# Retention fetches the next head pair ahead, and the output projection's first tiles take the contraction row by row

## The chip, the cores and the metric

The kernel runs on one core of a Trainium2 chip. The metric is the device time of one execution in microseconds (us), given as the median of several runs. The engines named below are PE (TensorE, the matmuls), DVE (VectorE), ACT (ScalarE), POOL (GpSimd) and SP (SyncE, whose queue issues nearly all transfers).

## The reference, cut to what matters

Two layers work on 256 context tokens and 512 latent tokens of width 1024. In each, one input projection feeds four mixers (RWKV, SSD, Hyena, retention) of width 512; each mixer's gated output is projected, weighted by a sigmoid gate of the layer's input, added up, and projected once more. The change touches retention and the output projection. Retention goes in chunks of 128 tokens, for 8 heads of 64, forwards and backwards:

```python
def step(s, inp):
    qc, kc, vc = inp
    att = jnp.einsum('bnhd,bmhd->bhnm', qc, kc) * inner
    y = jnp.einsum('bhnm,bmhe->bnhe', att, vc)
    y = y + jnp.einsum('bnhd,bhde->bnhe', qc, s) * xi[None, :, :, None]
    s = g_chunk[None, :, None, None] * s + jnp.einsum('bmhd,bmhe,hm->bhde', kc, vc, zeta)
    return s, y
```

q and k pass a rotary embedding before it; y passes a norm over each head and a SiLU gate behind it.

## The kernel before

**Dense work.** Every projection in fp32 is three matmuls: both factors are split into a high and a low part (`uh`, `ul` for the layer's input, `yh`, `yl` for a mixer's output, `whi`, `wlo` for a weight tile), and hi·hi, lo·hi and hi·lo are added in PSUM. The helper of L215 issues these "dense" matmuls; each works on 512 latent columns (`dl`) or 256 context columns (`dc`). A weight tile is fetched by L193 (`wraw`), its high part cast by ACT (L185), its low part made by DVE (L186).

**Who sets the order.** The code gives the work in program order; the tile framework's list scheduler fixes at build time the order in which each engine and queue runs it. Each engine then runs its list strictly in turn. Dense work of the merge, which stands behind retention in the code, is thereby put between the steps of the mixers; it needs weight tiles from SP's queue. Tiles with the same tag share a fixed number of buffers (`BUFS`), and a transfer into one waits until its last reader is done.

**Retention.** `ret` calls `ret_ct` for four pairs of heads, pair 0 to pair 3. A pair fetches q, k and v from DRAM (L477), turns q and k (L961 to L964 on DVE), transposes v and k on PE (`cen`, `ident`, L174), scales k (`kz`, L983 on DVE), makes the chunk states (`vt`·`kz` on PE, `S`, L1008 and L1011 on DVE), multiplies q by k on PE, weights the products (`att`, L1026 on DVE) and adds both parts up in PSUM (`sy`, L174). The head norm follows: a square on ACT, a matmul with `bones` (L386), DVE's L397 to L400, then the gate (L403) and the store of `yd` (L1040). Layer 0 does it for 768 tokens, layer 1 for 512 outputs. The merge of mixer 3 reads `yd` of all four pairs back.

**Output projection.** `outp` works in four column blocks j; each splits four weight tiles (`owh`, `owl`, the fourth in `whi`, `wlo`), and for each 128-row tile (six in layer 0, four in layer 1) adds 24 matmuls of 256 columns (L1284 to L1286) in one of three PSUM buffers `o`. DVE's L1289 (`ot`) reads such a buffer and frees it.

Of the kernel before, what the change touches and what calls it, by code (L numbers as in the profile page):

```python
# [17 lines left out]
T_LAT, T_CTX, T = 512, 256, 768  # L18
# [121 lines left out]
class K:  # L140
# [5 lines left out]
    def tile(self, pool, shape, dt=F32, tag=None, bufs=None):  # L146
        self.n += 1
        kw = {}
        bufs = bufs or self.BUFS.get(tag)
        if bufs is not None:  # L150
            kw["bufs"] = bufs
        return pool.tile(shape, dt, tag=tag, name=f"{tag}_{self.n}", **kw)

    BUFS = dict(KB=1, pc=2, late=1, y=1, bonus=1, gt=4, stc=10, S=6, att=2, zn=2, yh=1, yl=1,  mg=2, rt2=5, rt=2, st=5, E=3, m2=2, cbm=2, dd=2, xd=2, sd=1, yo=1, ub=2, hw=2, ha=2, heo=1,
                H=2, Hs=1, eo=1, eot=1, U=2, Yf=1, t1=1, ss=1, et=3, AR=3, KBt=2, vt=2, UV=2, Rs=1, Z=2, pcm=1, wraw512=2, whi512=3, wlo512=3, fg=3, fh=3, hx=3, fraw=1, xh=1, xl=1,
                ht=2, hsq=1, hnm=1, hss=4, uf=2, uc0=1, hn=6, ot=2, adr=4, adh=3, adl=3, owh=5, owl=5)
    PSUM_D = dict(dl=2, dc=1)
# [771 lines left out]
    def ret(self, l, need_ctx, p):  # L929
        tc, V, S, G = self.tc, self.V, self.S, self.G  # L930
        segs = [(0, 512), (512, 256)]
        osegs = segs if need_ctx else segs[:1]
        self.load_smask(p)
        ld = {}
        for n, sh in (("dif", [128, 2, 128]), ("xidx", [128, 2, 128]), ("zidx", [128, 2]), ("rope", [128, 2, 512])):
            ld[n] = self.tile(p, sh, F32, n)
            self.nc.sync.dma_start(out=ld[n][:], in_=self.a[n])
        Dm = self.tile(p, [128, 8, 128], F32, "Dm")
        D2 = self.tile(p, [128, 8, 128], F32, "D2")
        for d, t in ((0, Dm), (1, D2)):  # L940
            for h in range(8):
                S.activation(out=t[:, h, :], in_=ld["dif"][:, d, :], func=AF.Exp, scale=self.col("lgr", 8 * d + h))
            G.tensor_tensor(out=t[:], in0=t[:], in1=self.smask[:, d, :].unsqueeze(1).to_broadcast([128, 8, 128]), op=ALU.mult)
        V.tensor_tensor(out=Dm[:], in0=Dm[:], in1=D2[:], op=ALU.add)
        zeta = self.tile(p, [128, 2, 8], F32, "zeta")
        for d in range(2):
            S.activation(out=zeta[:, d, :], in_=self.col("lgr", 8 * d, 8), func=AF.Exp, scale=ld["zidx"][:, d:d + 1])
        gch = self.tile(p, [128, 8], F32, "gch")
        S.activation(out=gch[:], in_=self.col("lg", 0, 8), func=AF.Exp, scale=128.0)
        for ct in range(4):  # L950
            self.ret_ct(l, ct, need_ctx, p, segs, osegs, ld, Dm, zeta, gch)

    def ret_ct(self, l, ct, need_ctx, p, segs, osegs, ld, Dm, zeta, gch):
        V, S, G = self.V, self.S, self.G
        no = T if need_ctx else 512
        nch = 6 if need_ctx else 4

        def rope(x):
            sh = self.tile(p, [128, 512], F32, "rt")
            mask = [(i + 16) % 32 for i in range(32)]  # L960
            V.stream_shuffle(out=sh[:], in_=x[:, 0:512], mask=mask)  # L961
            V.tensor_tensor(out=sh[:], in0=sh[:], in1=ld["rope"][:, 1, :], op=ALU.mult)
            V.tensor_tensor(out=x[:, 0:512], in0=x[:, 0:512], in1=ld["rope"][:, 0, :], op=ALU.mult)
            V.tensor_tensor(out=x[:, 0:512], in0=x[:, 0:512], in1=sh[:], op=ALU.add)  # L964

        q = self.fetch(l, "rq", ct, no, p, "q")
        k = self.fetch(l, "rk", ct, T, p, "k")
        v = self.fetch(l, "rv", ct, T, p, "rt2")
        rope(q)
        rope(k)  # L970
        vt = self.tile(p, [128, 6, 128], F32, "vt")
# [1 line left out]
        for src, kind in ((v, 0), (k, 1)):  # L973
            for gq in range(2):
                ps = self.ps("s", [128, 3, 128])
# [37 lines left out]
        y = self.tile(p, [128, T], F32, "rt2")  # L1013
        for t0, n in osegs:
# [3 lines left out]
            for b in range(nb):  # L1018
                o = t0 + b * 128
# [3 lines left out]
            att = []  # L1023
# [232 lines left out]
    def outp(self, l, need_ctx, acc, ah, p, wp, done):  # L1256

        V, nc = self.V, self.nc
        no = T if need_ctx else 512
        nt = no // 128  # L1260
        lag = 2 if need_ctx else 0
        al = self.tile(p, [128, 8, T], F32R, "al")
        for oc in range(8):
            self.split(ah[:, oc, :no], al[:, oc, :no], acc[:, oc, :no], scale=0.5)
        gb = self.tile(p, [128, 2, D], F32, "gb")
        for s in range(2 if need_ctx else 1):
            g = self.modd[l].rearrange("(c s) x -> c s x", s=2)[:, s, :]
            nc.sync.dma_start(out=gb[:, s, :], in_=bass.AP(g.tensor, g.offset, [[0, 128]] + list(g.ap)))
        hn = [self.tile(p, [128, D], F32, "hn") for _ in range(nt)]
        for i in range(nt):  # L1270
            nc.sync.dma_start(out=hn[i][:], in_=self.h_in(l, i))
        for j in range(4):
            w = []
            for q in range(4):
                raw = self.tile(self.wpool, [128, 2, 256], F32, "wraw512")
                nc.sync.dma_start(out=raw[:], in_=self.a["out_w"][l, j, :, 2 * q:2 * q + 2])
                hi, lo = (self.tile(self.wpool if q == 3 else wp, [128, 2, 256], F32R, t) for t in (("whi512", "wlo512") if q == 3 else ("owh", "owl")))
                self.split(hi[:], lo[:], raw[:])
                w += [(hi[:, kk, :], lo[:, kk, :]) for kk in range(2)]
            for i in range(nt):  # L1280
                ps = self.pst("o", [128, 256])
                ac = slice(i * 128, (i + 1) * 128)
                for k in range(8):
                    self.P.matmul(ps[:], ah[:, k, ac], w[k][0], start=(k == 0), stop=False)  # L1284
                    self.P.matmul(ps[:], al[:, k, ac], w[k][0], start=False, stop=False)  # L1285
                    self.P.matmul(ps[:], ah[:, k, ac], w[k][1], start=False, stop=(k == 7))  # L1286
                t = self.tile(p, [128, 256], F32, "ot")
                cs = slice(j * 256, (j + 1) * 256)
                V.tensor_tensor(out=t[:], in0=ps[:], in1=gb[:, 0 if i < 4 else 1, cs], op=ALU.mult)  # L1289
                V.tensor_tensor(out=hn[i][:, cs], in0=hn[i][:, cs], in1=t[:], op=ALU.add)  # L1290
                if j == 3 and i >= lag:
                    done(i - lag, hn[i - lag])
        for i in range(nt - lag, nt):
            done(i, hn[i])
# [179 lines left out]
```

## Time and profile before

| | |
|---|---|
| median of 3 runs | 3001.47 us (2997.48 to 3002.77) |
| the profiled execution | 3006.24 us |
| its span, first to last instruction | 3004.4 us |
| mean granted TensorE clock | 0.978 |
| PE busy | 2841.8 us, 95% of the span |
| PE's weight loads busy | 2294.0 us, 76% |
| DVE busy | 1906.4 us, 63% |
| ACT busy | 1187.5 us, 40% |
| POOL busy | 456.7 us, 15% |

Spans and rows are of the profiled execution; 1.84 us of its time lie outside its span. Its time is 4.77 us above the median of the runs. Busy PE time holds matmuls that wait in the array's pipeline, and the clock is a share of 2.4 GHz: 0.50 means the level of 1.2 GHz.

### The profile page before, as it was taken

What the parts mean: (1) busy time and instruction counts of PE and PEld (TensorE: products, weight loads), DVE (VectorE), ACT (ScalarE), POOL (GpSimd) and SP (SyncE); (2) the same over time, 40 slices, a digit from 0 to 9 for tenths busy, and PEclk for the clock granted to TensorE, in tenths of its full rate; (3) what the DMA queues carried; (4) which work ended last, traced back from release to release, by engine and by line L of the source; (5) the groups of instructions that cost most, each with busy time, mean ns of one, the idle gap of its engine ahead of it and who ended that gap; (6) DMA issues with size and microseconds to landing.
All of it is one profiled execution on the core that took longest, in us unless ns stands there. A gap on an engine that the chain in (4) does not pass through costs nothing. (4 is left out here: it accounts for less than half of the span.)

```text
span 3004.4 us, 48440 instructions
## 1 busy us (share of the span) xinstructions
PE 2841.8 (95%) x18708; PEld 2294.0 (76%) x18708; DVE 1906.4 (63%) x3544; ACT 1187.5 (40%) x2109; POOL 456.7 (15%) x650
## 2 busy tenths in 40 slices
PE   7998999999999999999999989899999999999897
PEld 3787878787777887777778878777777788877677
DVE  3348575665636769876735446757576746787865
ACT  4643424333336323334532464334344443333432
POOL 2300202112010001210012230121212010021111
PEclk9999999999999999999999999899989999999999
DMA  6543213131216332233535354223222225333334
GB/s 195 192 135 105 96 64 97 63 104 45 92 56 228 122 124 79 87 112 121 169 123 172 97 196 144 74 79 116 71 99 81 70 83 170 124 105 101 123 118 138
DMA packets 164266, 343.24 MB, mean 114 GB/s; under 512 B 19105, under 2 KB 28130, under 8 KB 164036
## 3 DMA queue, kind: packets, MB, share of 16 engines
q1 hardware_dynamic: 164036, 340.15, 34.6%
q8 instruction: 147, 2.41, 0.3%
q14 instruction: 83, 0.68, 0.1%
HBM read 254.77 MB, written 83.74 MB: 113 GB/s over the span
## 5 line engine op out<-in xcount | busy, mean ns | idle before, releaser
L215 PE MATMUL dl<-uh,whi 128*128 128x512 f32 (+1 forms) x1520 | 621.6, 409 | 6.6 <-ACT fg L457 3.1
L215 PE MATMUL dl<-ul,whi 128*128 128x512 f32 (+1 forms) x1520 | 618.9, 407 | 2.6 <-DVE ul L379 2.5
L215 PE MATMUL dl<-uh,wlo 128*128 128x512 f32 (+1 forms) x1520 | 616.1, 405 | 2.3 <-DVE wlo L186 2.3
L185 ACT CAST whi<-wraw 128x512 fp32r<-128x512 f32 x452 | 278.2, 615 | 642.0 <-PE dc L215 281.8
L186 DVE TENSOR_TENSOR wlo<-wraw,whi 128x512 fp32r<-128x512 f32 x452 | 324.4, 718 | 290.1 <-ACT whi L185 251.6
L215 PEld LDWEIGHTS dl<-uh,wlo 128*128 128x128 f32 (+1 forms) x1520 | 288.2, 190 | 68.3 <-DVE wlo L186 4.4
L215 PEld LDWEIGHTS dl<-uh,whi 128*128 128x128 f32 (+1 forms) x1520 | 288.6, 190 | 67.0 <-ACT fg L457 3.9
L215 PEld LDWEIGHTS dl<-ul,whi 128*128 128x128 f32 (+1 forms) x1520 | 288.8, 190 | 62.3 <-DVE ul L379 6.5
L215 PE MATMUL dc<-uh,whi 128*128 128x256 f32 (+1 forms) x960 | 277.4, 289 | 6.1 <-DVE fg L446 3.1
L215 PE MATMUL dc<-ul,whi 128*128 128x256 f32 (+1 forms) x960 | 276.0, 288 | 1.9 <-DVE ul L379 1.9
L215 PE MATMUL dc<-uh,wlo 128*128 128x256 f32 (+1 forms) x960 | 274.3, 286 | 0.0
L215 PEld LDWEIGHTS dc<-uh,whi 128*128 128x128 f32 (+1 forms) x960 | 180.6, 188 | 22.6 <-DVE fg L446 4.4
L215 PEld LDWEIGHTS dc<-ul,whi 128*128 128x128 f32 (+1 forms) x960 | 180.4, 188 | 18.2 <-DVE ul L379 6.2
L215 PEld LDWEIGHTS dc<-uh,wlo 128*128 128x128 f32 (+1 forms) x960 | 180.2, 188 | 4.1 <-issue 1.1
L1252 POOL TENSOR_TENSOR acc<-acc,fg 128x512 f32<-128x512 f32 x72 | 92.5, 1294 | 502.9 <-DVE fg L1251 501.5
L728 DVE TENSOR_TENSOR Z<-cc,Z 128x256 f32<-128x256 f32 x80 | 33.8, 422 | 139.4 <-PE cc L174 138.8
L858 POOL TENSOR_TENSOR m<-smask,adl 128x512 fp32r<-128x512 f32 x24 | 34.0, 1415 | 537.2 <-DVE adl L186 410.1
L215 PE MATMUL dl<-yh,whi 128*128 128x512 f32 x256 | 104.0, 408 | 7.3 <-ACT yh L185 6.4
L215 PE MATMUL dl<-yl,whi 128*128 128x512 f32 x256 | 103.7, 406 | 2.6 <-DVE yl L186 2.6
L215 PE MATMUL dl<-yh,wlo 128*128 128x512 f32 x256 | 104.2, 408 | 0.0
L701 POOL COPY UV<-vt 64x128 f32<-64x128 f32 x192 | 76.7, 422 | 166.8 <-ACT vt L634 161.2
L713 ACT COPY Rs<-cc 64x256 f32<-64x256 f32 x96 | 35.3, 367 | 161.2 <-PE cc L174 160.3
(422 smaller groups left out, 5722.5 us busy)
## 6 DMA issues: line engine op xcount, KB each, us to landing
wraw<-in_w SPq DMA_DIRECT2D x248, 256.0 KB, 2.7
wraw<-merge_w SPq DMA_DIRECT2D x128, 256.0 KB, 2.7
adr<-ada_w SPq DMA_DIRECT2D x96, 256.0 KB, 3.6
wraw<-branch_w SPq DMA_DIRECT2D x64, 256.0 KB, 2.8
wraw<-out_w SPq DMA_DIRECT2D x32, 256.0 KB, 3.8
pdlw<-fg SPq DMA_DIRECT2D x16, 384.0 KB, 2.4
pdla<-fg SPq DMA_DIRECT2D x16, 384.0 KB, 2.9
hfd<-Hs SPq DMA_DIRECT2D x16, 384.0 KB, 2.9
```

The costliest lines, as they stand in the source:

```text
L185: (heng or self.S).copy(out=hi, in_=src) if heng is None else heng.tensor_copy(out=hi, in_=src)
L186: (leng or self.V).tensor_tensor(out=lo, in0=src, in1=hi.bitcast(F32), op=ALU.subtract)
L215: i = self.P.matmul(out[t0][:M, :n], w[:, kk, :], u[:, k, t0:t0 + n], start=(k == 0 and p == 0), stop=(k == nk - 1 and p == 2))
L701: G.tensor_copy(out=UV[hk, d], in_=vt[d][hk, slot[d] // 2, :].rearrange("p (h x) -> p h x", h=2))
L713: S.copy(out=Rs[hb], in_=Rp.t[hb])
L728: V.tensor_tensor(out=Zn[:], in0=Zp.t[:], in1=Z[:], op=ALU.add)
L858: eng.tensor_tensor(out=m2[:], in0=self.smask[:, d, :].unsqueeze(1).to_broadcast([128, 4, 128]), in1=ad[:, c, hs:hs + 4].bitcast(F32).unsq ...
L1252: G.tensor_tensor(out=acc[:, oc, t0:t0 + n], in0=acc[:, oc, t0:t0 + n], in1=g[:, t0:t0 + n], op=ALU.add)
```

## The change

In retention `ret` fetches q, k and v of pair 0, and those of pair n+1 ahead of the code of pair n. They have tags of their own: two buffers for q and for k, one for v. The tag `rt2` has four buffers instead of five. In `outp` the first three tiles of block j = 0 are written with the contraction index k outermost: rows k = 0 to 6 over the three tiles, then k = 7 tile by tile. For these PE keeps the order of the code. The arithmetic is the same.

```diff
-    BUFS = dict(... rt2=5, rt=2, ...
+    BUFS = dict(... rt2=4, q2=2, k2=2, v2=1, rt=2, ...
...
+        def get(ct):
+            return [self.fetch(l, nm, ct, n, p, tag) for nm, n, tag in (("rq", no, "q2"), ("rk", T, "k2"), ("rv", T, "v2"))]
+
+        nxt = get(0)
         for ct in range(4):
-            self.ret_ct(l, ct, need_ctx, p, segs, osegs, ld, Dm, zeta, gch)
+            qkv, nxt = nxt, get(ct + 1) if ct < 3 else None
+            self.ret_ct(l, ct, need_ctx, p, segs, osegs, ld, Dm, zeta, gch, *qkv)
...
-        q = self.fetch(l, "rq", ct, no, p, "q")
-        k = self.fetch(l, "rk", ct, T, p, "k")
-        v = self.fetch(l, "rv", ct, T, p, "rt2")
...
-            for i in range(nt):
-                ps = self.pst("o", [128, 256])
-                ac = slice(i * 128, (i + 1) * 128)
-                for k in range(8):
+            ahead = range(min(3, nt) if j == 0 else 0)
+            pss = {}
+            def rows(i, ks):
+                if i not in pss:
+                    pss[i] = self.pst("o", [128, 256])
+                ps, ac = pss[i], slice(i * 128, (i + 1) * 128)
+                for k in ks:
                     self.P.matmul(ps[:], ah[:, k, ac], w[k][0], start=(k == 0), stop=False)
...
+            if ahead:
+                with self.tc.manual_schedule(engines={mybir.EngineType.PE}):
+                    for k in range(7):
+                        for i in ahead:
+                            rows(i, [k])
+                    for i in ahead:
+                        rows(i, [7])
```

What this does to the engines' lists is seen at three places. The first is SP's queue in layer 1, from the fetch of pair 1 to the store of pair 0 (`q`, `k`, and `rt<-pdrv` are a pair's fetch, `wraw` weight tiles of the merge, `rt<-pdgr` the gate). Before:

```order
L477 DMA q_24674<-pdrq_24_92 128x512
L477 DMA k_24676<-pdrk_26_94 128x768
L193 DMA wraw_5112_26454<-merge_w 128x512
L193 DMA wraw_5117_26475<-branch_w 128x512
L193 DMA wraw_5121_26496<-merge_w 128x512
L477 DMA rt_4720_24670<-pdgr_34_102 128x512
L477 DMA rt_4723_24678<-pdrv_28_96 128x768
L193 DMA wraw_5124_26514<-merge_w 128x512
L193 DMA wraw_5129_26535<-branch_w 128x512
L1040 DMA yd_71<-rt_4711_24626 128x512
L193 DMA wraw_5133_26556<-merge_w 128x512
L477 DMA q_24803<-pdrq_24_92 128x512
```

And now, from v of pair 1 on (L1044 is the store, L1040 before):

```order
L477 DMA v_4691_24558<-pdrv_28_96 128x768
L477 DMA q_4724_24683<-pdrq_24_92 128x512
L477 DMA k_4725_24685<-pdrk_26_94 128x768
L477 DMA v_4726_24687<-pdrv_28_96 128x768
L477 DMA rt_4723_24679<-pdgr_34_102 128x512
L477 DMA q_4759_24812<-pdrq_24_92 128x512
L1044 DMA yd_71<-rt_4714_24635 128x512
L477 DMA k_4760_24814<-pdrk_26_94 128x768
L477 DMA v_4761_24816<-pdrv_28_96 128x768
L477 DMA rt_4758_24808<-pdgr_34_102 128x512
L1044 DMA yd_71<-rt_4749_24764 128x512
L193 DMA wraw_5112_26457<-merge_w 128x512
```

The five merge weight tiles that stood between the fetch of pair 1 and the store of pair 0 now stand behind the fetches of pairs 2 and 3 and the store of pair 1. Next is PE in layer 1, where pair 1 begins (`cen` and `ident` transpose v and k, `dl` rows are dense). Before, 35 dense rows run from the `bones` matmul of pair 0 to this place:

```order
L215 MATMUL dl_26435<-uh_15075,wlo_5114_26457 128x512
L215 MATMUL dl_26435<-uh_15075,whi_5113_26456 128x512
L174 MATMUL s_24693<-cen_116,rt_4723_24678 128x128 x3
L174 MATMUL s_24698<-cen_116,rt_4723_24678 128x128 x3
L174 MATMUL s_24703<-ident_112,k_24676 128x128 x3
L174 MATMUL s_24709<-ident_112,k_24676 128x128 x3
L215 MATMUL dl_26435<-ul_15076,whi_5113_26456 128x512
L215 MATMUL dl_26435<-uh_15075,wlo_5114_26457 128x512
L215 MATMUL dl_26474<-yh_26293,whi_5118_26477 128x512
L215 MATMUL dl_26474<-yl_26294,whi_5118_26477 128x512
L215 MATMUL dl_26474<-yh_26293,wlo_5119_26478 128x512
L174 MATMUL s_24722<-vt_24690,kz_4727_24691 128x128
```

And now, where pair 2 begins, from the last `sy` row of pair 1 on:

```order
L174 MATMUL sy_24765<-qx_4737_24727,S_24760 128x128
L174 MATMUL sy_24765<-qx_4738_24729,S_24739 128x128
L386 MATMUL s_24799<-rt_4755_24796,bones_114 128x512
L174 MATMUL s_24831<-cen_116,v_4726_24687 128x128 x3
L174 MATMUL s_24836<-cen_116,v_4726_24687 128x128 x3
L174 MATMUL s_24841<-ident_112,k_4725_24685 128x128 x3
L174 MATMUL s_24847<-ident_112,k_4725_24685 128x128 x3
L174 MATMUL s_24860<-vt_24828,kz_4765_24829 128x128
L174 MATMUL s_24865<-vt_24828,kz_4765_24829 128x128
L174 MATMUL s_24872<-vt_24828,kz_4765_24829 128x128
```

The dense rows ahead of the transposes and behind them are gone. From the first `sy` row of pair 0 to the first of pair 3, 183 dense rows stood in layer 1 before and 13 stand there now; the 170 others come behind pair 3. In layer 0 the pairs follow each other in the same way, but keep dense rows in between, except in pair 0: there 8 dense rows (6 of 512 columns, 2 of 256) stood between the q·k rows and the first `sy` row, 4 of 256 between the first two `sy` rows, 6 of 256 ahead of `bones`, and none stands there now. The third place is DVE in the output projection of layer 0, behind the last split of block 0 (`owl` are low parts for block 1). Before:

```order
L186 TENSOR_TENSOR wlo_2848_15140<-wraw_2846_15137,whi_2847_15139 128x512
L1289 TENSOR_TENSOR ot_15168<-o_15143,gb_15104 128x256
L1290 TENSOR_TENSOR hn_15107<-hn_15107,ot_15168 128x256
L186 TENSOR_TENSOR owl_15314<-wraw_2861_15311,owh_15313 128x512
L1289 TENSOR_TENSOR ot_15196<-o_15171,gb_15104 128x256
L186 TENSOR_TENSOR owl_15320<-wraw_2864_15317,owh_15319 128x512
L1290 TENSOR_TENSOR hn_15108<-hn_15108,ot_15196 128x256
L1289 TENSOR_TENSOR ot_15224<-o_15199,gb_15104 128x256
```

And now (L1310 and L1311 are `ot` and `hn`, L1289 and L1290 before):

```order
L186 TENSOR_TENSOR wlo_2848_15140<-wraw_2846_15137,whi_2847_15139 128x512
L186 TENSOR_TENSOR owl_15317<-wraw_2861_15314,owh_15316 128x512
L186 TENSOR_TENSOR owl_15323<-wraw_2864_15320,owh_15322 128x512
L1310 TENSOR_TENSOR ot_15221<-o_15145,gb_15104 128x256
L1310 TENSOR_TENSOR ot_15224<-o_15149,gb_15104 128x256
L1311 TENSOR_TENSOR hn_15107<-hn_15107,ot_15221 128x256
L1311 TENSOR_TENSOR hn_15108<-hn_15108,ot_15224 128x256
L1310 TENSOR_TENSOR ot_15227<-o_15153,gb_15104 128x256
```

The first `ot` stood ahead of both `owl` of the next block and stands behind them now; layer 1 has the same rows in the same two orders.

## Rows read from the trace of the kernel before

**Rows 1.** Stretches: from:to, length; busy us of PE, PEld, DVE, ACT, POOL; clock; DMA

```profile
1326.00:1418.00 92.00, 89.71 (x606) 73.84 (x604) 65.87 (x133) 39.82 (x74) 5.24 (x2) 1.00 0.38 127
2810.70:2892.50 81.80, 77.93 (x463) 60.65 (x462) 68.20 (x134) 30.08 (x45) 9.51 (x6) 1.00 0.34 108
2912.70:2919.60 6.90, 5.79 (x14) 4.58 (x15) 3.03 (x4) 1.24 (x2) 0.51 (x1) 0.51 0.64 196
2920.00:2937.90 17.90, 17.90 (x79) 14.55 (x78) 9.29 (x12) 3.73 (x6) 9.80 (x7) 1.00 0.59 177
```

**Rows 2.** What VectorE waited for, layer 0 retention, 1326 to 1425 us

```profile
DVE rt L961 <- DMA q<-pdrq: 8.6, 4, 4.1
```

**Rows 3.** SP's queue in layer 1 (start, us, line, transfer)

```profile
2811.29 0.33 SPq L193 DMA_DIRECT2D wraw<-merge_w  x1
2835.30 0.33 SPq L477 DMA_DIRECT2D q<-pdrq  x1
```

**Rows 4.** TensorE by line in layer 1, 2810.7 to 2892.5 us

```profile
L215 PE MATMUL dl<-uh,wlo 128*128 128x512 f32 x41 | 17.0, 415 | 0.0
L215 PE MATMUL dl<-yh,wlo 128*128 128x512 f32 x20 | 8.4, 422 | 0.0
```

**Rows 5.** Timeline of VectorE in layer 1, pair 0 to pair 1, and pair 3

```profile
2809.38 1.28 DVE L1026 TENSOR_TENSOR att<-s,Dm 128x512 f32<-128x512 f32 x2
2817.11 0.69 DVE L397 TENSOR_SCALAR rt<-s 128x512 f32<-128x512 f32 x1 [1.61 <-PE s L386]
2819.52 0.68 DVE L992 TENSOR_TENSOR qx<-q,xi 128x512 f32<-128x512 f32 x1
2823.74 0.68 DVE L400 TENSOR_TENSOR rt<-sy,rt 128x512 f32<-128x512 f32 x1
2830.03 1.95 DVE L983 TENSOR_TENSOR kz<-s,zeta 128x384 f32<-128x384 f32 x4 [2.50 <-PE s L174]
2832.84 1.09 DVE L1008 TENSOR_TENSOR S<-s,bones 128x256 f32<-128x256 f32 x3 [0.25 <-PE s L174]
2836.60 1.28 DVE L1026 TENSOR_TENSOR att<-s,Dm 128x512 f32<-128x512 f32 x2
2891.78 1.27 DVE L1026 TENSOR_TENSOR att<-s,Dm 128x512 f32<-128x512 f32 x2
```

**Rows 6.** TensorE in layer 1: twelve transposes of pairs 0 and 1

```profile
2792.41 2.93 PE L174 MATMUL s<-cen,rt 128*128 128x128 f32 x12 [1.51 <-DMA rt<-pdrv]
2827.83 1.50 PE L174 MATMUL s<-cen,rt 128*128 128x128 f32 x12
```

**Rows 7.** What TensorE waited for behind pair 3, 2892 to 2930 us

```profile
PE dl L215 <- ACT yh L185: 1.8, 1, 1.8
PE dl L215 <- DVE yl L186: 1.3, 1, 1.3
```

**Rows 8.** Timeline of TensorE in layer 0, pair 0

```profile
1346.70 0.51 PE L215 MATMUL dl<-uh,whi 128*128 128x512 f32 x1
1348.66 0.43 PE L174 MATMUL sy<-att,vt 128*64 128x128 f32 x2
```

**Rows 9.** Output projection, layer 0: TensorE's fourth tile, VectorE's first split

```profile
1632.34 0.28 PE L1284 MATMUL o<-owh,ah 128*128 128x256 f32 x1
1632.46 0.28 PE L1285 MATMUL o<-owh,al 128*128 128x256 f32 x1
1633.25 0.69 DVE L186 TENSOR_TENSOR owl<-wraw,owh 128x512 fp32r<-128x512 f32 x1 [2.59 <-ACT owh L185]
```

**Rows 10.** The same in layer 1, and TensorE's wait behind it

```profile
2953.20 0.28 PE L1284 MATMUL o<-owh,ah 128*128 128x256 f32 x1
2954.29 0.69 DVE L186 TENSOR_TENSOR owl<-wraw,owh 128x512 fp32r<-128x512 f32 x1 [2.76 <-ACT owh L185]
PE o L1284 <- ACT owh L185: 1.4, 2, 1.0
```

More of the change, by code (lines that the diff above doesn't have):

```diff
@@ L152, in tile @@
         return pool.tile(shape, dt, tag=tag, name=f"{tag}_{self.n}", **kw)
-    BUFS = dict(KB=1, pc=2, late=1, y=1, bonus=1, gt=4, stc=10, S=6, att=2, zn=2, yh=1, yl=1,  mg=2, rt2=5, rt=2, st=5, E=3, m2=2, cbm=2, dd=2, xd=2, sd=1, yo=1, ub=2, hw=2, ha=2, heo=1,
+    BUFS = dict(KB=1, pc=2, late=1, y=1, bonus=1, gt=4, stc=10, S=6, att=2, zn=2, yh=1, yl=1,  mg=2, rt2=4, q2=2, k2=2, v2=1, rt=2, st=5, E=3, m2=2, cbm=2, dd=2, xd=2, sd=1, yo=1, ub=2, hw=2, ha=2, heo=1,
                 H=2, Hs=1, eo=1, eot=1, U=2, Yf=1, t1=1, ss=1, et=3, AR=3, KBt=2, vt=2, UV=2, Rs=1, Z=2, pcm=1, wraw512=2, whi512=3, wlo512=3, fg=3, fh=3, hx=3, fraw=1, xh=1, xl=1,
@@ L949, in ret, with ret_ct @@
         S.activation(out=gch[:], in_=self.col("lg", 0, 8), func=AF.Exp, scale=128.0)
+        no = T if need_ctx else 512
+        def get(ct):
+            return [self.fetch(l, nm, ct, n, p, tag) for nm, n, tag in (("rq", no, "q2"), ("rk", T, "k2"), ("rv", T, "v2"))]
+        nxt = get(0)
         for ct in range(4):
-            self.ret_ct(l, ct, need_ctx, p, segs, osegs, ld, Dm, zeta, gch)
-    def ret_ct(self, l, ct, need_ctx, p, segs, osegs, ld, Dm, zeta, gch):
+            qkv, nxt = nxt, get(ct + 1) if ct < 3 else None
+            self.ret_ct(l, ct, need_ctx, p, segs, osegs, ld, Dm, zeta, gch, *qkv)
+    def ret_ct(self, l, ct, need_ctx, p, segs, osegs, ld, Dm, zeta, gch, q, k, v):
         V, S, G = self.V, self.S, self.G
@@ L1286, in outp @@
                     self.P.matmul(ps[:], ah[:, k, ac], w[k][1], start=False, stop=(k == 7))
+            if ahead:
[5 more added lines that the diff above has]
+                        rows(i, [7])
+            for i in range(nt):
+                if i not in ahead:
+                    rows(i, range(8))
+                ps = pss[i]
                 t = self.tile(p, [128, 256], F32, "ot")
```

## The prediction

> **What bounds the kernel now.** I read the windows view first. TensorE (PE) is the engine that everything waits for: in layer 0's retention it is busy 89.71 of 92.00 us, in layer 1 from the last `att` row of pair 0 to that of pair 3 it is busy 77.93 of 81.80 us, both at the full clock [rows 1]. So whatever the change saves by shorter waits of other engines, it can save in these stretches no more than PE's own idle time: 2.29 and 3.87 us. Next come the waits of DVE: it waited 8.6 us for q in layer 0 [rows 2]. That looks like the prize, but PE had dense rows to run meanwhile, so little of it was on the path. The lines view shows what covered it in layer 1: 3 x 41 + 3 x 20 = 183 dense matmuls [rows 4] of 0.2266 us each (79 in 17.90 us at the full clock [rows 1]), 41.5 us of the 77.93. Retention's own matmuls are the other 36.4 us, 12.1 us a pair. The work of the pair that PE waits for is DVE's, so its timeline comes last, below.
>
> **Layer 1: dense rows leave the pairs.** The lists show 170 of the 183 dense rows moved behind pair 3. They are not saved; they cost 170 x 0.2266 = 38.5 us there. What counts is how long a pair takes without them. DVE's own list for one pair, from its timeline [rows 5]: the block of `S`, its updates and `att` runs 2832.84 to 2837.88, 5.0 us; four `kz` 1.95 us; and 16 wide operations (eight of the two rotations, two `qx`, L397, L279 to L281, L400, L403), each 0.603 us (seven from 2819.52 to 2823.74), 9.65 us. Together 16.6 us, more than PE's 12.1. On top come waits: in pair 1 DVE waited 1.61 us ahead of L397, 2.50 ahead of `kz` and 0.25 ahead of `S` [rows 5], 4.4 us, because norm, transposes and state are a ring between PE, ACT and DVE. The rotations of the next pair, whose q and k are now there, fill part of these. A pair thus takes 16.6 to 21.0 us; I take 18.0, a third of the waits.
>
> PE then idles some 18.0 - 12.1 = 5.9 us in each pair, and its clock may fall. The trace has one such place: behind pair 3 PE waited 1.8 and then 1.3 us [rows 7], and the stretch behind it ran at a granted clock of 0.51, the level of 1.2 GHz [rows 1]. What that costs: twelve transposes took 1.50 us at the full clock and 2.93 at the low level [rows 6], 1.43 us more. I take one low stretch a pair, long enough for its 24 transposes: 2.9 us, so a pair of 20.9 us. The ends are none (18.0) and the whole of a pair's own matmuls: 12.1 us more, of which the 5.9 us of idle time can hide that much, so 24.2 to 30.1 us a pair.
>
> The Trainium skill, page "TensorE: Matmul & The Clock Gate", Part 1, calls the low level the default state, left by activity and fallen back into by idling. The rows behind pair 3 agree with it. By it alone the pairs would run wholly at 1.2 GHz, and the sum would be that of the second rival below.
>
> Against this stands a gain: the 3.1 us of waits behind pair 3 [rows 7] were there because merge 3 needs `yd` of pair 3 back and nothing else was left to run. With 38.5 us of dense rows in that place they go, and so does the low stretch: 14 matmuls were busy 5.79 us where 14 x 0.2266 = 3.2 us do, 2.6 us [rows 1]. Together 5.7 us.
>
> Sum for layer 1: 3 x 20.9 + 38.5 = 101.2 us against 81.8, +19.4, less 5.7: **+13.7**. With pairs of 18.0: 92.5, less 5.7, +5.0. At the least 3 x 16.6 + 38.5 = 88.3, +6.5 - 5.7 = +0.8. At the low level throughout +23.6 (24.2 us a pair) to +41.3 (30.1).
>
> **SP's queue.** The twelve fetches of a layer stay twelve; only their places change. Before, a weight tile left at 2811.29 and the fetch of pair 2 at 2835.30 [rows 3]; now five weight tiles stand behind it. With one buffer for v, the fetch of v of pair 2 waits until PE has transposed pair 1's, and q of pair 3, the store of pair 0 and the weight tiles behind them wait in turn. The price is nothing as long as PE asks for no new weight tile in the pairs; the lists have 13 dense rows there, on tiles fetched earlier. If it did, the wait would be PE's own, and it is inside the upper ends. `rt2` with one buffer less could hold up the norm of the next pair; that wait too lies in the 4.4 us of ring.
>
> **Layer 0.** Pair 0 loses its cover. Before, the eight dense rows and no idle time filled the 1.96 us between the q·k rows and `sy` (1346.70 to 1348.66) [rows 8], in which DVE finished `S` and `att`. The ten rows of 256 columns that followed are worth 10 x 0.12 = 1.2 us (pitch from [rows 9]), and covered the second `att` and the square: 3.2 us idle now. The later pairs keep dense rows; a pair idled 2.29 / 4 = 0.6 us, and with less distance between the pairs I let each of three idle as much again, 1.8 us. **+5.0**. Ends: -2.3, if the fetch waits were all of PE's idle time, and 4 x 3.2 = +12.8, if every pair loses its cover as pair 0 does.
>
> **Output projection.** Taking k outermost lets the first rows of three tiles run while later splits are still made, but all three tiles then end together, and DVE's list puts `ot` of tile 1 behind two low parts of the next block. In layer 0 tile 4 began at 1632.34; the first of these splits began at 1633.25 [rows 9], when its high part was there. Back to back, at 0.603 us each [rows 5], the two are done near 1634.5, and `ot`, half as wide (0.4 us, an estimate from the 0.603), near 1634.9. PE has three buffers and they are full: **+2.6**. In layer 1 tile 4 began at 2953.20, the first split at 2954.29 [rows 10]; two splits and an `ot` later it is 2955.9, 2.7 us on. There PE waited 1.4 us for high parts [rows 10], which is partly repaid by a later arrival: **+1.3**. Ends: -1.4, if only those waits shrink, and +5.3.
>
> **The sum.** 13.7 + 5.0 + 2.6 + 1.3 = +22.6 us. The profiled execution's 3006.24 us become 3028.8; it lay 4.77 us above the median, so the median of 3001.47 becomes 3024.
>
> **The rivals.**
> *Faster, because the waits go.* PE's idle time in both stretches (2.29 + 3.87) and the 5.7 us behind pair 3 come back, 11.9 us, less 3.9 in the output projection: -8.0, 2993.5 us. DVE's 8.6 us wait for q speaks for it. Against it: it needs pairs shorter than (81.8 + 5.7 - 38.5) / 3 = 16.3 us for layer 1 to gain at all, and DVE's own list is 16.6. The Trainium skill, page "Trainium Kernel Development and Optimization", Best Practices, has the rule behind this rival, to double-buffer and overlap transfers with compute. The rows show the overlap was there already, by dense rows. Chance 0.08.
> *The low clock throughout layer 1's pairs.* +23.6 to +41.3 and the other 8.9: 3034 to 3052 us. The rows at 0.51 speak for it, and that PE would idle three times in each pair; against it, that its bursts in between are two thirds of the time. Chance 0.15.
> *Nothing to be seen.* Pairs at DVE's 16.6 us (+0.8), layer 0 unchanged, and the output projection at a third of its price: about 3003 us. For it speaks that all moved dense work is still done at the full clock; it needs the ring of waits hidden entirely. Chance 0.17.
> *The forecast*, pairs of 18.0 to 20.9 us with the rest as above: 3015 to 3024 us, to 3034 with the upper ends of layer 0 and of the output projection. Chance 0.60, nearer 3024 because the one place with such idle times did lose its clock.
>
> **Range and chances.** 3004 to 3044 us leaves out the faster rival, part of the rival of no change, and the upper half of the low clock. About 0.2% (6 us) is what a measurement of this kernel can tell from no change: faster 0.08, within it 0.17, slower 0.75.
>
> **What would show it.** After: in layer 1 the `att` rows of pairs 0 and 3 lie 54 to 63 us apart, with PE busy about two thirds of that at a clock below 1, then a stretch of dense rows without idle time, and no wait of merge 3. The q waits of L961 vanish. In layer 0 PE idles some 2 us between q·k and `sy` of pair 0. Tile 4 of both output projections waits for `ot`. I am wrong if pairs come under 16.3 us, if DVE interleaves the two pairs so that the ring overlaps, or if layer 0's later stretches had idle time of PE that the moved dense rows fill.

## The result, and the profile after

The changed kernel takes 3040.38 us (median of 4 runs, 3037.52 to 3041.28) against 3000.68 for the kernel before: a ratio of 1.0126, interval 1.0112 to 1.0139, so about 40 us slower. The profiled execution has a span of 3039.5 us against 3004.4, and a mean granted clock of 0.969 against 0.978.

Where the 35.1 us of span arose is read from two transfers that stand at the same place in both programs: `dif` at the start of each retention, and the first `out_w` of each output projection. SP's timeline, before and then after (start, length, line, transfer):

```profile
1324.42 0.33 SPq L937 DMA_DIRECT2D dif<-dif  x1
1603.42 0.38 SPq L1276 DMA_DIRECT2D wraw<-out_w  x1
2783.09 0.33 SPq L937 DMA_DIRECT2D dif<-dif  x1
2930.98 0.33 SPq L1276 DMA_DIRECT2D wraw<-out_w  x1
```

```profile
1323.13 0.33 SPq L937 DMA_DIRECT2D dif<-dif  x1
1611.41 1.04 SPq L1280 DMA_DIRECT2D wraw<-out_w  x1
2793.36 0.33 SPq L937 DMA_DIRECT2D dif<-dif  x1
2966.01 0.33 SPq L1280 DMA_DIRECT2D wraw<-out_w  x1
```

Up to the retention of layer 0, where nothing was changed, this execution is 1.3 us ahead. From there to the output projection it takes 288.28 us instead of 279.00, **+9.3**. From that projection, which is part of the change, through to layer 1's retention it loses 2.3 more. Layer 1's retention and merges take 172.65 us instead of 147.89, **+24.8**. Behind that nothing is added. The windows view of the kernel after, in the columns of [rows 1]: the stretch of layer 0's pairs, layer 1 from the end of `att` of pair 0 to that of pair 3, two low stretches in it, the dense rows behind pair 3 up to `out_w`, the low stretch at their head, and the one at merge 3:

```profile
1324.60:1420.00 95.40, 90.46 (x583) 72.46 (x581) 73.58 (x148) 37.63 (x71) 5.24 (x2) 0.95 0.36 122
2820.78:2885.57 64.79, 51.39 (x295) 38.48 (x295) 50.59 (x111) 17.78 (x26) 0.00 (x0) 0.79 0.18 58
2837.30:2851.00 13.70, 11.56 (x43) 7.84 (x44) 8.57 (x19) 1.30 (x3) 0.00 (x0) 0.50 0.21 65
2861.20:2874.90 13.70, 12.54 (x48) 8.82 (x49) 7.82 (x14) 1.94 (x3) 0.00 (x0) 0.50 0.02 3
2885.57:2966.01 80.44, 77.02 (x318) 60.53 (x319) 34.07 (x50) 24.43 (x39) 19.32 (x12) 0.92 0.38 115
2885.10:2895.30 10.20, 9.67 (x37) 6.78 (x37) 3.00 (x5) 1.83 (x3) 0.41 (x1) 0.50 0.01 2
2950.00:2953.40 3.40, 3.08 (x7) 2.51 (x8) 1.26 (x3) 1.02 (x2) 0.00 (x0) 0.50 0.72 222
```

Layer 1's three pairs take 64.79 us, 21.6 each, where the same piece took 82.39 with the dense rows in it (2810.66 to 2893.05, the ends of the `att` rows of pairs 0 and 3 [rows 5]; the window of [rows 1] stops 0.55 us short of that). PE is busy 51.39 of that, and the clock is 0.79: two stretches of 13.7 us were granted 0.50, the level of 1.2 GHz. The dense rows then run 80.44 us, where before 37.93 us lay between pair 3 and `out_w`:

```profile
2893.05:2930.98 37.93, 34.88 (x149) 26.53 (x150) 18.79 (x27) 13.41 (x20) 9.29 (x6) 0.91 0.44 139
```

So 17.6 us are gained in the pairs and 42.5 are lost behind them, which is the 24.8 above but for 0.1. What PE waited for in the pairs (us in all, times, longest):

```profile
PE sy L174 <- DVE att L1030: 7.7, 5, 2.3
PE s L174 <- DVE kz L987: 2.9, 2, 1.6
PE s L386 <- ACT rt L394: 1.6, 3, 0.7
```

No single wait is longer than 2.3 us.

### The profile page after: what moved, and what is told of

Its sections match the earlier page's. It is cut to its first block, busy times and chain, and to the rows that moved or that the text cites. A ratio compares the mean times of both kernels' runs of the same rounds, so it can differ in the third digit from the quotient of the medians.

```text
span 3039.5 us, 48441 instructions
## 1 busy us (share of the span) xinstructions
PE 2862.4 (94%) x18708; PEld 2312.1 (76%) x18708; DVE 1903.7 (63%) x3544; ACT 1178.2 (39%) x2103; POOL 456.9 (15%) x650
## 5 line engine op out<-in xcount | busy, mean ns | idle before, releaser
L185 ACT CAST whi<-wraw 128x512 fp32r<-128x512 f32 x452 | 278.2, 615 | 638.6 <-PE dc L215 279.0
L215 PEld LDWEIGHTS dc<-uh,whi 128*128 128x128 f32 (+1 forms) x960 | 181.5, 189 | 24.8 <-DVE fg L446 4.5
```

The costliest lines, as they stand in the source:

```text
L185: (heng or self.S).copy(out=hi, in_=src) if heng is None else heng.tensor_copy(out=hi, in_=src)
L215: i = self.P.matmul(out[t0][:M, :n], w[:, kk, :], u[:, k, t0:t0 + n], start=(k == 0 and p == 0), stop=(k == nk - 1 and p == 2))
```

## The experiments

All were timed against the kernel before, and ratios are to it; a ratio of 0.001 is 3 us.

**e1_fetch_only**: the retention of the change, `outp` of before.

> Retention as in the changed kernel, the output projection as before. If the loss is the dense rows that left the pairs (theory), nearly all of it stays: 33 to 38 us above before, with the same 65 us from att of pair 0 to att of pair 3 in layer 1. If the output projection and the low clock behind it are the larger part (rival), under 20 us.

Measured: 1.0119 (1.0098 to 1.0141), 36 us. The loss is retention's, and the first `sy` rows of pairs 0 and 3 lie 64.8 us apart here too (2819.46 to 2884.24).

**e2_outp_only**: `outp` of the change, retention of before.

> The output projection as in the changed kernel, retention as before. Theory: 2 to 5 us above before, from PE's wait of about 2.3 us for ot ahead of the fourth tile in each layer and a low clock behind it. Rival (the output projection is the larger part): over 15 us. A third way, that the order of rows is worth something by itself: at or below before.

Measured: 1.0011 (1.0000 to 1.0022), 3 us, with an interval that begins at none. PE waits for `ot` in both layers, 2.3 us in layer 0; in layer 1:

```profile
PE o L1289 <- DVE ot L1306: 2.4, 1, 2.4
```

**e3_fetch_l0** and **e4_fetch_l1**: fetching ahead in one layer alone, `outp` of before.

```diff
+        ahead = l == 0      # e3;   l == 1 in e4
+        self.BUFS = dict(self.BUFS, rt2=4 if ahead else 5)
-        nxt = get(0)
+        nxt = get(0) if ahead else None
         for ct in range(4):
-            qkv, nxt = nxt, get(ct + 1) if ct < 3 else None
+            if ahead:
+                qkv, nxt = nxt, get(ct + 1) if ct < 3 else None
+            else:
+                qkv = [self.fetch(l, "rq", ct, no, p, "q"), self.fetch(l, "rk", ct, T, p, "k"), self.fetch(l, "rv", ct, T, p, "rt2")]
```

> Fetching ahead in layer 0 alone, all else as before; pair 0 of layer 0 loses its dense rows, the other pairs keep about 60 each. Theory: 8 to 12 us above before, of which 5 to 6 are a low clock in pair 0. If fetching ahead helps where dense rows stay (the rival of step 1, waits go): below before.

> Fetching ahead in layer 1 alone, all else as before; 13 dense rows are left from the first sy row of pair 0 to that of pair 3. Theory: 23 to 28 us above before, pairs of 21 to 22 us with a mean granted clock of about 0.8. If the loss were in the queue or in the transfers themselves, it would be split evenly over the two layers: about 17 us.

Measured: e3 1.0027 (1.0016 to 1.0038), 8 us; e4 1.0088 (1.0069 to 1.0106), 26 us. With e2's 3 us that makes 1.0126, the change's own ratio: the parts add up. The transfers are the same twelve in each layer and the losses are three to one, so they don't follow the number of transfers. They go the way of the dense rows that left the space between the first `sy` rows of pairs 0 and 3: 170 in layer 1, and in layer 0, counted in the same way, 48 of 512 columns and 60 of 256, worth 78. That is two to one, not three; the granted clock in the pairs fell further in layer 1 as well (0.79 against 0.95). In e4 layer 1 shows the changed kernel again, 65.30 us at 0.79 for the pairs, and 173.9 us from `dif` (2783.74) to `out_w` (2957.66):

```profile
2811.80:2877.10 65.30, 51.65 (x295) 38.93 (x295) 50.62 (x112) 17.79 (x26) 0.00 (x0) 0.79 0.17 57
```

In layer 0 of e3, `dif` to `out_w` takes 288.82 us, as after the change:

```profile
1322.95 0.33 SPq L937 DMA_DIRECT2D dif<-dif  x1
1611.77 0.89 SPq L1285 DMA_DIRECT2D wraw<-out_w  x1
```

**e5_fetch_held**: everything fetched ahead, but the next pair's first rotation is held on DVE behind the gate of the pair before. Both operations are DVE's, so this sets nothing but an order; the scheduler then puts 70 to 73 dense rows between the pairs of layer 1.

```diff
-            V.stream_shuffle(out=sh[:], in_=x[:, 0:512], mask=mask)
+            i = V.stream_shuffle(out=sh[:], in_=x[:, 0:512], mask=mask)
+            if ct and not self.held:
+                self.held = True
+                self.tc.add_manual_dep(i.ins, self.gated, NOSYNC, reason="pair order")
...
+        self.gated = self.apply_gate(self.fetch(l, "gr", ct, no, p, "rt2"), y, no).ins.name
```

> All fetches ahead as in the changed kernel, but the first rotation of a pair is held on DVE until the gate of the pair before; that leaves 70 to 73 dense rows between the pairs of layer 1 (54 to 66 before the change). Output projection as before. Theory (the lost cover costs, not the fetch): the loss goes, -4 to +4 us against before. Rival (the fetches, their place in SP's queue or their buffers cost): it stays 20 us or more above before.

Measured: 1.0030 (1.0019 to 1.0041), 9 us: 27 of e1's 36 us come back, but more than theory's bound of 4 us stays. The windows of the pairs and of what follows them, and PE's waits behind the pairs, show where:

```profile
2811.90:2902.40 90.50, 86.07 (x498) 67.19 (x499) 67.08 (x137) 32.21 (x49) 8.82 (x6) 1.00 0.28 90
2902.40:2950.00 47.60, 37.08 (x151) 27.53 (x151) 24.59 (x33) 12.86 (x21) 14.81 (x10) 0.89 0.54 169
PE dl L215 <- ACT yh L185: 5.0, 2, 3.7
PE dl L215 <- DVE yl L186: 2.3, 1, 2.3
```

With the same fetches the clock in the pairs is 1.00 and PE is busy 86.07 of 90.50 us. But 215 dense rows are now inside the pairs instead of 183, fewer are left behind them, and PE waits 7.3 us for the split outputs of the merge there, where it waited 3.1 before the change [rows 7]. From `dif` to `out_w` layer 1 takes 153.73 us (2784.38 to 2938.11) against 147.89 before. So in the pairs the fetch is harmless: with the dense rows kept between them, the low clock is gone and three quarters of the loss with it. That the 9 us left come from the rows that now stand too early is read from these rows; it was not tried.

**f_after**: the changed kernel with 14 matmuls of 256 columns more in each pair of layer 1, read by nothing. Each is two rows in the trace.

```diff
+        if not need_ctx:
+            for _ in range(6):
+                self.P.matmul(self.dcb[:, 1, :], self.ident[:], k[:, :256], start=True, stop=True)
...
+            if not need_ctx:
+                for _ in range(8):
+                    self.P.matmul(self.dcb[:, 0, :], self.ident[:], qx[0][:, :256], start=True, stop=True)
```

> The changed kernel with 14 added matmuls of 256 columns in each pair of layer 1, whose results nothing reads: 6 behind the transposes, 8 behind the q and k products, where PE waits for DVE. Theory (PE's idle time makes the clock fall, and the low clock makes half of the loss in the pairs): the granted clock from pair 0 to pair 3 rises from 0.79 to 0.9 or more, a pair falls from 21.6 us to under 20.5 though PE has more to do, and the time is 3 to 12 us below the changed kernel (28 to 37 us above before). Rival (the clock follows from something else, or has no price): the added work costs its 2 to 4 us a pair, 6 us or more above the changed kernel.

Measured: 1.0118 (1.0103 to 1.0132), 35 us above before: inside theory's 28 to 37, but the interval overlaps the change's own, so the total doesn't show a gain. The stretch does. The window of the three pairs, and the added rows in it:

```profile
2824.96:2882.94 57.98, 57.87 (x382) 46.10 (x381) 50.51 (x110) 17.71 (x26) 1.27 (x1) 1.00 0.18 62
L1032 PE MATMUL dc<-qx,ident 128*128 128x256 f32 x54 | 13.9, 388 | 0.0
L991 PE MATMUL dc<-k,ident 128*128 128x256 f32 x36 | 8.8, 380 | 0.0
```

The clock is 1.00 throughout, and the pairs take 57.98 us, 19.3 each, instead of 64.79, although 90 added rows (22.7 us busy; six of them still belong to pair 0) run in them. PE is busy 57.87 us of that. From `dif` to `out_w` layer 1 takes 166.05 us (2796.40 to 2962.45) instead of 172.65. The scheduler left 7 dense rows in the pairs instead of 13, 1.4 us, so the low clock costs at least 5.4 us here; and it is PE's idle time that brings it: with that time filled, the clock stays.

**e6_outp_ot_first**: e2 with an order on DVE: the first low part of block 1 stands behind `ot` of the third tile.

```diff
+                lo_ = self.split(hi[:], lo[:], raw[:])
+                if j == 1 and q == 0:
+                    self.tc.add_manual_dep(lo_.ins, self.ots, NOSYNC, reason="ot first")
...
+                if j == 0 and i in (0, 1, 2):
+                    self.ots = o_.ins.name
```

> Output projection as in the changed kernel, but with DVE reading out the first three tiles before the low parts of the next block; retention as before. Theory (the wait for ot behind the two low parts is the price): PE's wait of about 2.3 us ahead of the fourth tile falls under 0.8 us in both layers, and the time is within 2 us of before. Rival (three tiles that end together cost by themselves, whatever DVE does): a wait of 1.5 us or more stays.

Measured: 1.0001 (0.9992 to 1.0010). The wait for `ot` is gone in both layers; in layer 1's projection PE waits for the input's high part, as it did before the change, and for nothing else longer than 0.3 us:

```profile
PE o L1291 <- ACT ah L188: 3.2, 1, 3.2
```

Taking the contraction row by row shows neither gain nor loss here, and the order of `ot` was what PE waited for. That its 3 us came back is not shown by time alone: the interval overlaps e2's.

**y3_before, y3_after, y4_before, y4_after**: the kernels before and after, with tiles of their own in merge 3 for `yh` and `yl` (y3), and for the four loaded pieces of `yd` as well (y4).

```diff
-        yh = self.tile(p, [128, 4, T], F32R, "yh")
-        yl = self.tile(p, [128, 4, T], F32R, "yl")
+        yp = self.apool if m == 3 else p
+        yh = self.tile(yp, [128, 4, T], F32R, "yh")
+        yl = self.tile(yp, [128, 4, T], F32R, "yl")
...
-            yr = self.tile(self.fpool, [128, T], F32, "fg")
+            yr = self.tile(self.apool, [128, T], F32, "yr3", bufs=4) if m == 3 else self.tile(self.fpool, [128, T], F32, "fg")
```

> The kernel before, with tiles of their own for the split outputs yh and yl of merge 3. If PE's waits ahead of merge 3 come from the single buffer of yh and yl (theory, new), they go: PE waits under 0.8 us there instead of 3.1 in layer 1, and the time falls by 3 to 8 us. If they come from the late yd of pair 3 (the step of the prediction), nothing changes.

> The changed kernel, with tiles of their own for yh and yl of merge 3. Theory: the waits ahead of merge 3, which the change did not remove, go here too, and the time falls by 3 to 8 us against the changed kernel, to 32 to 37 us above before. If late yd of pair 3 were the cause, they would already be gone in the changed kernel, and nothing changes.

> The kernel before, with tiles of their own in merge 3 for yh, yl and for the four pieces of yd that it loads. If the three buffers fg make PE wait ahead of merge 3 (theory), those waits fall from 3.1 us in layer 1 to under 1 us and the time by 2 to 6 us. If ACT's order makes them (rival: the split waits behind a weight cast), 1.5 us or more stays and the time is within 2 us of before.

> The changed kernel, with tiles of their own in merge 3 for yh, yl and the four pieces of yd that it loads. Where yd of pair 3 is stored some 38 us before merge 3 reads it, and the three buffers fg are what is left to wait for (theory), PE's waits of 1.0 and 1.4 us ahead of merge 3 in layer 1 go with the low clock behind them, and the time is 3 to 7 us below the changed kernel, 33 to 37 us above before. If yd itself were late there too, or ACT's order held the split (rival), waits of 2 us or more stay.

Measured: y3_before 0.9995 (0.9986 to 1.0004), y3_after 1.0101 (1.0083 to 1.0119), y4_before 0.9994 (0.9982 to 1.0005), y4_after 1.0084 (1.0072 to 1.0097). The first three theories failed. The buffers `yh` and `yl` alone change nothing at merge 3: PE still waited 1.8 and 1.2 us there in y3_before, and in y3_after 1.0 and 1.4 as in the changed kernel. With all tiles of its own the kernel before waits in another way, longer and in one piece, from the store of `yd` of pair 3 to its arrival. The rival's sign, that the wait stays, came, but not for its reason: ahead of the split ACT waited 5.28 us for the transfer, and not behind a weight cast:

```profile
PE dl L215 <- ACT yh L185: 7.2, 1, 7.2
2903.14 0.32 SPq L1040 DMA_DIRECT2D yd<-rt  x1
2906.62 1.85 SPq L1234 DMA_DIRECT2D yr<-yd  x4
2909.57 0.62 ACT L185 CAST yh<-yr 128x512 fp32r<-128x512 f32 x1 [5.28 <-DMA yr<-yd]
```

In the changed kernel, with 38 us of dense rows ahead of merge 3, the same edit takes the waits away. The loads leave right behind the store (2906.33) instead of 38 us later, the granted clock stays at 1.00 from 2940 to 2963, and PE's waits between pair 3 and the output projection of y4_after are these, none for `yh` or `yl`:

```profile
2908.70 1.37 SPq L1238 DMA_DIRECT2D yr<-yd  x3
PE sy L174 <- DVE att L1030: 3.0, 2, 2.3
PE dl L215 <- ACT fg L1226: 1.0, 1, 1.0
PE dl L215 <- DVE fg L1256: 0.7, 1, 0.7
```

So both reasons held, one behind the other: late `yd` before the change, the three buffers `fg` after it. y4_after gains 12 us on the change by its runs, more than theory's 3 to 7. Its profile shows 2.9 of them in layer 1 (169.71 us from `dif` to `out_w`, 2793.32 to 2963.03) and 5.7 in layer 0 (282.61 us, 1327.88 to 1610.49, against 288.28). How much of this is the waits' worth stays open: y3_after, which kept them, came out 8 us under the changed kernel too, with overlapping intervals.

**qk_ahead**: q and k fetched ahead, v at the head of its pair as before.

```diff
-            return [self.fetch(l, nm, ct, n, p, tag) for nm, n, tag in (("rq", no, "q2"), ("rk", T, "k2"), ("rv", T, "v2"))]
+            return [self.fetch(l, nm, ct, n, p, tag) for nm, n, tag in (("rq", no, "q2"), ("rk", T, "k2"))]
...
+        v = self.fetch(l, "rv", ct, T, p, "rt2")
         rope(q)
```

> q and k fetched ahead as in the changed kernel, v fetched at the head of its pair as before, output projection as before. In layer 1 this leaves 24, 65 and 60 dense rows between the pairs (54, 63 and 66 before the change, 6, 0 and 7 with it). Theory (time follows the dense rows that cover the pairs): 0 to 7 us above before, with one short interval between pairs 0 and 1. Rival (fetching q and k ahead costs by itself): 15 us or more.

Measured: 1.0049 (1.0035 to 1.0063), 15 us, 11 to 19 by the interval. The theory's 0 to 7 us is missed. The rival's bound of 15 us lies inside the interval, so the time alone doesn't refuse it. Layer 1 takes 162.04 us from `dif` to `out_w` (2785.51 to 2947.55), 14 more than before. Its pairs, and PE's two longest waits for dense work in them:

```profile
2814.10:2902.40 88.30, 77.28 (x432) 59.12 (x433) 65.56 (x130) 28.91 (x43) 7.94 (x5) 0.90 0.24 81
PE dl L215 <- ACT fg L1227: 4.5, 1, 4.5
PE dl L215 <- DVE wlo L186: 2.2, 1, 2.2
```

The three pairs take 88.3 us at 0.90 with only 149 dense rows in them. Both waits are between pairs 0 and 1: 4.5 us for a gate `fg` and 2.2 for a weight tile's low part. Neither was for a transfer: the low part was made at 2828.42 from a tile that SP had issued by 2790.51. ACT ran without a pause from 2820.51 to the gate, and DVE from 2818.57 to the low part, with rotations of q and k that were fetched ahead in its list. The number of dense rows is thus not all that counts; what ACT and DVE do ahead of them counts too. How much of the 15 us this makes was not tried.

No version here is faster than the kernel before by more than its interval.

## Why the prediction was right, point by point

The direction, the place and the mechanism held: the dense rows moved behind pair 3, PE ran short of work in the pairs, and its clock fell. The size did not hold as well. It came out at 40 us where 23 were forecast: 3040 us is inside the range of 3004 to 3044, but above the forecast's own band, which ended at 3034, and in the band of the second rival (3034 to 3052). The range holds it because it was drawn half way into that rival; that much is luck. In layer 1 alone 24.8 us were lost where 13.7 were forecast, 2.1 of the difference in the pairs and 9.7 behind them. By its steps:

- **Pairs of 20.9 us** became 21.6, and the `att` rows of pairs 0 and 3 lie 64.8 us apart, where 54 to 63 were forecast. The three are not alike (each from the end of one pair's `att` to that of the next):

```profile
2820.78:2839.39 18.61, 14.25 (x100) 10.53 (x100) 16.97 (x39) 7.36 (x11) 0.00 (x0) 0.94 0.25 78
2839.39:2862.23 22.84, 17.63 (x94) 13.17 (x94) 16.85 (x38) 6.25 (x9) 0.00 (x0) 0.72 0.17 56
2862.23:2885.57 23.34, 19.52 (x101) 14.78 (x101) 16.76 (x36) 4.17 (x6) 0.00 (x0) 0.72 0.14 45
```

DVE is busy 16.8 to 17.0 us in each, near the forecast's 16.6. Pair 1 takes 18.6 us, near the forecast's 18.0 without a low stretch. Pairs 2 and 3 hold most of one each and take 4.2 and 4.7 us more, where 2.9 were forecast: this term was too small. The low stretch was mis-placed, too: it was forecast over 24 transposes, and lies over the `sy` rows, the `bones` matmul and the transposes of v, 13.7 us long. f_after bounds the price of the two from below at 5.4 us; the forecast had 8.6 for three. PE idled 4.5 us in each pair (64.79 less 51.39, by three) against 5.9.
- **38.5 us for the moved rows** held, but the stretch behind pair 3 grew by 42.5, because its first 10.2 us still ran at 0.50. This is the third low stretch: it begins with the wait for pair 3's `att` and so falls behind the pairs, where the prediction had none. Its price is about 4.8 us, an estimate: half of 9.67 us busy.
- **The gain of 5.7 us at merge 3** failed as a step. PE waited there after the change too, 3.4 us in all, and the low stretch of 2950.0 to 2953.4 followed, some 1.5 us (half of 3.08 busy). Against the 5.7 us of before, 0.8 were gained; 38.5 and 4.8 less 0.8 are the 42.5. The waits behind pair 3 up to the output projection:

```profile
PE dl L215 <- DVE yl L186: 1.4, 1, 1.4
PE dl L215 <- ACT yh L185: 1.0, 1, 1.0
PE dl L215 <- ACT fg L1226: 1.0, 1, 1.0
```

The store of `yd` of pair 3 was early, as forecast, but the loads came 38 us later in two halves:

```profile
2904.85 0.33 SPq L1044 DMA_DIRECT2D yd<-rt  x1
2943.23 0.90 SPq L1237 DMA_DIRECT2D fg<-yd  x2
2949.74 0.87 SPq L1237 DMA_DIRECT2D fg<-yd  x2
```

The prediction took the cause of the wait before the change for the only one. y4_after shows the second, the three buffers `fg`.
- **Layer 0, +5.0**, measured +9.3 in the profile and 8 us in e3. Profiles of this stretch scatter: from `dif` to `out_w` it takes 279.0 to 283.7 us in four kernels with the retention of before in layer 0 (before, e2, e4, e6), and 287.7 to 290.3 in five that fetch ahead there (the change, e1, e3, f_after, y3_after). The lost cover of pair 0 was sized well: PE waited 2.11 us for `att`, as forecast near 1.96, and 0.69 for the square.

```profile
1349.10:1359.30 10.20, 9.51 (x37) 5.92 (x36) 5.45 (x11) 3.02 (x4) 0.00 (x0) 0.50 0.22 56
1347.32 0.43 PE L174 MATMUL sy<-att,vt 128*64 128x128 f32 x2 [2.11 <-DVE att L1030]
1354.87 2.07 PE L386 MATMUL s<-rt,bones 128*128 128x512 f32 x2 [0.69 <-ACT rt L394]
```

PE's idle time in the pairs rose by 2.7 us only, from 2.29 [rows 1] to 4.94 (95.40 less 90.46), though more rows left than pair 0's: 108 between the first `sy` rows of pairs 0 and 3, as counted above. What was missing is the clock: behind the 2.11 us it fell, and the `sy` and `bones` rows from 1349.1 to 1359.3 ran at a granted 0.50, the first row above; half of 9.51 us busy is 4.8 us, an estimate of its price. The fetch waits did not vanish as forecast either; DVE still waited 5.6 us for q in layer 0, 4.1 of them in one piece for pair 0's (at 1329.34), which nothing fetches earlier:

```profile
DVE rt L968 <- DMA q<-pdrq: 5.6, 3, 4.1
```

- **Output projection, +2.6 and +1.3.** PE's fourth tile waited 2.36 us in layer 0 and 2.10 in layer 1 for `ot`:

```profile
1642.97 0.58 PE L1293 MATMUL o<-owh,ah 128*128 128x256 f32 x1 [2.36 <-DVE ot L1310]
2990.27 0.39 PE L1293 MATMUL o<-owh,ah 128*128 128x256 f32 x1 [2.10 <-DVE ot L1310]
```

In layer 0 it is the two low parts ahead of `ot` on DVE that end late, at 1642.5:

```profile
1641.25 1.34 DVE L186 TENSOR_TENSOR owl<-wraw,owh 128x512 fp32r<-128x512 f32 x2 [4.43 <-ACT owh L185]
1642.50 0.75 DVE L1310 TENSOR_TENSOR ot<-o,gb 128x256 f32<-128x256 f32 x2
```

e2 puts both layers together at 3 us, against 3.9. In the profile of the change layer 1 shows none of its 1.3: from `out_w` to the end of the span it takes 73.49 us, against 73.42 before.
- **The rivals.** That the waits go would have shown as a gain in e3, where some two thirds of the dense rows stay; it lost 8 us. The low clock throughout the pairs came half true: two stretches of 13.7 us in the 65 us of the pairs, and one of 10.2 behind. Its time came out, but not its way: the clock was back at 1.00 from 2851.0 to 2861.2, and the pairs took 64.8 us where the forecast had 62.7 and this rival 72.6 or more. The Trainium skill, page "TensorE: Matmul & The Clock Gate", Part 1, says that idling brings the low level and activity lifts it; f_after agrees, with 0.79 and 1.00 for the same pairs.

## What to carry to other kernels

Where PE is the bound, a wait of another engine that PE covers with other work is free, and taking it away lets a list scheduler spend the cover elsewhere: read from the order how much independent work stands between the dependent steps before and after. Price such a move by the longest engine's own list for one step, plus the moved work at its full price, plus the low clock in and behind the bare stretch. When a wait has a cause, look for the next one before counting it as gained.

## What the runs showed of the hardware

PE's clock fell although no wait in layer 1's pairs was longer than 2.3 us, and in layer 0 behind one of 2.11 us; before the change, behind waits of 1.8 and 1.3 us [rows 7], it fell too [rows 1]. Work that nothing reads made the stretch shorter: 90 added rows raised the granted clock from 0.79 to 1.00 and cut 64.79 us to 57.98.
